# One more up-projection tile by Strassen's scheme, and coarser turns in the attention

## The chip, the cores and the metric

The kernel runs on one core of a Trainium2 chip. The metric is device time in microseconds (us), median of three runs. The core has TensorE (PE: matmuls, results in PSUM banks of 128 x 512 words), VectorE (DVE) and ScalarE (ACT, activations with a scale and a running sum), GpSimd (POOL, which here issues DMAs and does little arithmetic) and SyncE (SP, which issues the weight loads). All DMA queues share 16 DMA engines.

## What is computed

One decoder block on 512 tokens of width 1024, in float32:

```python
proj = rmsnorm(x) @ w_in
o_a = nsa_mixer(q, k_c, v_c, k_s, v_s, k_w, v_w, nsa_gate)  # 8 query heads, 2 KV groups
o_b = rwkv7_mixer(rwkv_in)
merged = sigmoid(gate_a) * (o_a @ w_proj_a) + sigmoid(gate_b) * (o_b @ w_proj_b)
x = x + merged @ w_out
u = rmsnorm(x) @ w_up                    # 1024 x 5632: value and gate, 2816 columns each
val, gate = split(causal_conv3(u))
return x + (silu(gate) * val) @ w_down
```

The attention mixer adds three branches for each query head, each with its gate: a softmax over 31 compressed blocks, one over selected tokens and one over a window; with 512 tokens the last two see every earlier token.

## The kernel before

**Numbers.** Every weight and activation is split into two parts, `hi` (rounded to TensorE's fast 32-bit type) and `lo` (the rest); a product is three matmuls: hi by hi, lo by hi, hi by lo. For each weight tile SP loads `raw` (three buffers, `wload`), ACT makes `whi`, DVE makes `wlo` (`wsplit`, two buffers each). A `raw` buffer is free, and the load of the tile three places on is issued, when `wlo` of its tile has been made. `wnext` always splits one tile ahead of the one that TensorE uses. The order of the tiles is that of the generator `weight_tiles`.

**Attention** (lines 1240 to 1411). The twelve entries of `units` are (query tile qt, KV group, branches): eight with one branch, for qt 3 and 2, and four with both, for qt 1 and 0. `scores(u)` makes the scores of four heads in groups of one PSUM bank (tag `a`, two buffers): TensorE writes `ps_a`, DVE adds the bias table and takes the maximum (line 1314, output `P`, `nm`), ACT takes the exponential. The generator yields after each group; before the yield it issues DVE's pending scalings of the unit before (`pend`, one piece per group: rows of `P` times `sm`, line 135) and `filler(n)` matmuls of the two dense projections (`obT`, weights `w_proj_b`), which keep TensorE busy. `turns(u)` transposes the finished `P` in sets of four 128 x 128 blocks (line 1349) into one of three banks and copies each set out (`PTs`), three by ACT to one by DVE. The main loop alternates: one set of transposes of unit j, one group of scores of unit j + 2. Then `values` multiplies by V. `compressed(qt)` is the compressed branch's softmax: eight small matmuls (`KC`), ten steps of DVE on `sC` and an exponential; `compressed_t` transposes it. The order of TensorE's and GpSimd's instructions is that of the code here; DVE's and ACT's is chosen when the program is built.

**Merge** (after line 1415). For m in 0 to 7, TensorE multiplies `oaT` by one 128-column tile of `w_proj_a` (12 matmuls); then comes `w_out`.

**MLP** (from line 1515). 22 tiles f of 128 value and 128 gate columns. A dense tile is 2 x 24 matmuls of 128 x 512. For f in `SF` (4 to 15) `up_strassen` uses seven products of half size in place of eight, 7 x 12 matmuls of 128 x 256 (line 1613). It needs two kinds of sums. Sums of weight blocks are formed beforehand in memory, `usum`, by `sums_in_memory` on GpSimd's queue during the attention: 16 copies (line 243) and 16 accumulating DMAs (line 246), each over the `SF` columns of 128 rows. Sums of token blocks, `up_tokens` (tiles `Hw`, split into `R1M` and `R3Q`), are made by DVE and ACT while the dense tiles f = 0 to 3 run, two steps per tile. The first products of a Strassen tile need, in this order, the blocks H00 and H01 of the plain activations, then M2, R1 and R3 of the sums.

The functions that the change touches:

Of the kernel before, what the change touches and what calls it, by code (L numbers as in the profile page):

```python
# [22 lines left out]
KT = D // 128  # L23
DH = 64
H = 8
# [10 lines left out]
NGA = 1  # L36
NGB = 7
DECAY = math.exp(-0.5)
SF = range(4, 16)

O_Q, O_KC, O_VC, O_KS, O_VS, O_KW, O_VW, O_GATE, O_RWKV, O_GA, O_GB = (
    0, 512, 640, 768, 896, 1024, 1152, 1280, 1304, 3096, 4120)
# [42 lines left out]
def hybrid_block(ctx: ExitStack, tc: tile.TileContext, A: dict, out: bass.AP):  # L85
# [164 lines left out]
    def weight_tiles():  # L250
# [48 lines left out]
        for f in list(SF) + [None]:  # L299
# [8 lines left out]
                stream.append(up_block(p, 1, 1))  # L308
            if f is not None:
                stream += [up_sum(f, TS1), up_sum(f, TS3)]  # L310
        for i in range(0, len(stream) - 2, 2):
            yield stream[i:i + 2], KT, 128, v
        yield cols(A["w_up"][0], DFF + 128 * (SF[-1] + 1))
        yield stream[-2:], KT, 128, v
# [978 lines left out]
    def scores(u, n):  # L1293
        qt, g, bs = u
        qs = slice(128 * qt, 128 * qt + 128)
        N = 128 * (qt + 1)
        B = len(bs)
        P = Pb[units.index(u) % 4][:, 0:4 * B * N].rearrange("p (b r n) -> p b r n", b=B, n=N)
        nm = at.tile([128, 8], F32, name="nm", tag="nm", bufs=2)
        sm = at.tile([128, 8], F32, name="sm", tag="sm", bufs=2)  # L1300
        per = 512 // (B * N)
        todo, pend[:] = list(pend), []
        ng = 4 // per
        for r0 in range(0, 4, per):
            sp = pa()[:, 0:per * B * N].rearrange("p (r b n) -> p r b n", r=per, b=B)
            for r in range(r0, r0 + per):
                h = 4 * g + r
                for i, K in enumerate((KH, KL)):
                    mm(sp[:, r - r0], qst[:, h, qs], K[:, bs[0]:bs[0] + B, g, 0:N], i == 0, i == 1)
            for r in range(r0, r0 + per):  # L1310
                h = 4 * g + r
                for b in range(B):
                    i = 4 * b + r
                    v.tensor_tensor_reduce(out=P[:, b, r], in0=sp[:, r - r0, b], in1=BT[:, h, 384 - 128 * qt:512],  # L1314
                                           scale=-1.0, scalar=-NEG, op0=ALU.add, op1=ALU.min, accum_out=nm[:, i:i + 1])
                    act(P[:, b, r], P[:, b, r], AF.Exp, scale=-1.0, bias=nm[:, i:i + 1], accum_out=sm[:, i:i + 1])
            ig = r0 // per
            for f in todo[len(todo) * ig // ng:len(todo) * (ig + 1) // ng]:
                f()
            filler(n * (r0 + per) // 4 - n * r0 // 4)  # L1320
            yield
        v.reciprocal(sm[:, 0:4 * B], sm[:, 0:4 * B])
        for x, b in enumerate(bs):
            tt(sm[:, 4 * x:4 * x + 4], sm[:, 4 * x:4 * x + 4], gts[:, qt, 12 * g + 1 + b:12 * g + 12:3], ALU.mult)
        def row(b, r):
            i = 4 * b + r
            if r == 3:
                act(P[:, b, r], P[:, b, r], AF.Copy, scale=sm[:, i:i + 1])
            else:
                ts(P[:, b, r], P[:, b, r], sm[:, i:i + 1], None)  # L1330

        def branch(b):
            tt(P[:, b], P[:, b], sm[:, 4 * b:4 * b + 4, None].to_broadcast([128, 4, N]), ALU.mult)

        if B > 1:
            pend.append(lambda: branch(1))
        pend.extend(lambda r=r: row(0, r) for r in range(4))
        Ps[u] = P
# [50 lines left out]
    with tc.manual_schedule(engines=KTS):  # L1389
        run(scores(units[0], 12))  # L1390
        compressed(3)
        run(scores(units[1], 16))
        for i in range(0, len(units), 2):
            if i in (4, 8, 10):
                compressed_t(units[i][0])
            for j in (i, i + 1):
                a, b = turns(units[j]), scores(units[j + 2], nfill[j]) if j + 2 < len(units) else dense_only(nfill[j])
                alive = [a, b]
                while alive:
                    for x in list(alive):  # L1400
                        if next(x, alive) is alive:
                            alive.remove(x)
                    if j == 1 and len(PTk[units[1]]) == 2:
                        compressed_t(3)
            for j in (i, i + 1):
                values(units[j])
            for j in (i, i + 1):
                output(units[j])
            if i in (0, 4, 6):
                compressed({0: 2, 4: 1, 6: 0}[i])  # L1410
        filler(100)
    dbg("oaT", oaT.bitcast(F32))

# [185 lines left out]

    wpart = []  # L1600

    def up_weight():
        if not wpart:
            hi, lo = wnext(KT, 128)
            wpart.extend((hi[:, 4 * i:4 * i + 4], lo[:, 4 * i:4 * i + 4]) for i in range(2))
        return wpart.pop(0)

    def up_product(bank_, x, first=False):

        hi, lo = up_weight()  # L1610
        for k in range(8):
            for y in x[:2 - k // 4]:
                te.matmul(bank_, lhsT=(hi, lo)[k // 4][:, k % 4], rhs=y[:, k % 4], start=first and k == 0 and y is x[0],  # L1613
# [15 lines left out]
    def up_strassen():  # L1629
# [4 lines left out]
        for f in list(SF) + [None]:  # L1634
            if f is not None:
                B1 = mmb()[:, b0]
                up_product(B1, H[0][0], True)
                u = [us[:, 3 * (f % 2) + k] for k in range(3)]
                Cg, Cv = craw[f % 2], craw[2 + f % 2]
                act(u[0], B1)  # L1640
# [29 lines left out]
    for f in range(NF):  # L1670
# [15 lines left out]
        if f // 2 < PD:  # L1686
            cv = conv(dense_fm(hh, hl) if f else lead[1], f, 2 + f % 2)
            gate_value(f, cg, cv)
            for _ in range(2):
                next(side, None)  # L1690
            continue
        act(cg, cg, AF.Silu)
# [232 lines left out]
```

## Time and profile before

| what | us |
|---|---|
| median of three runs | 803.11 (802.75 to 803.26) |
| the profiled execution | 802.89 |
| its span, first to last instruction | 801.1 |
| outside the span | 1.8 |
| TensorE busy | 790.1 |
| VectorE busy | 642.1 |
| ScalarE busy | 482.8 |
| TensorE's granted clock | 1.00 throughout (2.4 GHz) |

Times in rows are microseconds from the span's start. Matmuls overlap: the length of one reaches into the next, so what an instruction costs is read from the distance of two starts. The same holds for DVE and ACT, whose lengths contain some 0.08 us of overlap. The attention runs from about 296 to 390 us, the merge to 412, the MLP from 459.

### The profile page before, as it was taken

The page shows a single profiled execution, that of the slowest core. Times are in us where ns is not written, and L with a number is a line of the kernel's source. Part 1 is how long each engine was busy: PE and PEld are TensorE (multiplying, and loading weights), DVE is VectorE, ACT ScalarE, POOL GpSimd, SP SyncE. Part 2 cuts the span into 40 slices and gives each one's busy share as a digit, 9 for nine tenths or more (in the row PEclk, how much of TensorE's full clock was granted, in tenths as well). Part 3 has the DMA queues.
Part 4 walks back from the last instruction along what each step waited for, and adds up shares of the span by engine and source line. Part 5 has one row for each costly group of instructions (what it writes and reads, how often), then busy time and mean ns, then how long its engine had stood idle before and what let it go on. Part 6 is the DMA issues. An engine that isn't in the chain of part 4 may idle for free.

```text
span 801.1 us, 14229 instructions
## 1 busy us (share of the span) xinstructions
PE 790.1 (99%) x5439; PEld 668.5 (83%) x5439; DVE 642.1 (80%) x1179; ACT 482.8 (60%) x929; POOL 92.8 (12%) x125
## 2 busy tenths in 40 slices
PE   7999999999999999999999999999999999999998
PEld 6788888887777887877788888999999888888886
DVE  4688899974565679888585489688898999989997
ACT  6777765454455678787344366677777754553452
POOL 5300021142000052221000000000000000002101
PEclk9999999999999999999999999999999999999999
DMA  7432323337362389999957134566666422584654
GB/s 221 125 90 68 99 74 105 86 101 210 80 132 54 79 227 271 261 261 269 196 183 243 50 133 118 154 185 182 173 184 182 128 79 80 181 309 167 234 179 153
DMA packets 138185, 126.27 MB, mean 158 GB/s; under 512 B 5806, under 2 KB 116069, under 8 KB 137989
## 3 DMA queue, kind: packets, MB, share of 16 engines
q1 hardware_dynamic: 123744, 83.21, 36.1%
q0 software_dynamic: 13312, 39.61, 18.5%
q10 hardware_dynamic: 1060, 2.55, 1.1%
q8 instruction: 42, 0.69, 0.4%
q14 instruction: 27, 0.21, 0.1%
HBM read 119.91 MB, written 29.56 MB: 187 GB/s over the span
## 4 chain that ended last, share of the span: by engine, by line
PE 90%; DVE 4%; DMA 4%; ACT 1%; issue 0%; POOL 0%; DVEq 0%
PE ps_mm L125 60%; PE ps_mm L1613 8%; PE ps_a L125 7%; PE ps_b L125 5%; PE ps_b L1613 4%; DMA usum<-in_w_up_dram 3%; PE ps_a L1613 2%; PE ps_b L1349 1%; DVE wlo L366 1%; PE ps_mm L1349 1%; DMA kc<-in_consts_dram 1%; DVE raw L131 0%; ACT whi L128 0%; PE ps_b L404 0%; PE ps_b L663 0%
## 5 line engine op out<-in xcount | busy, mean ns | idle before, releaser
L128 ACT ACTIVATE whi<-raw 128x1024 fp32r<-128x1024 f32 (+2 forms) x148 | 147.7, 999 | 129.9 <-PE ps_mm L125 61.0
L366 DVE TENSOR_TENSOR wlo<-raw,whi 128x1024 fp32r<-128x1024 f32 (+1 forms) x133 | 152.9, 1151 | 47.0 <-ACT whi L128 27.2
L125 PE MATMUL ps_mm<-hh,whi 128*128 128x512 f32 (+1 forms) x432 | 167.7, 391 | 0.3 <-ACT whi L128 0.2
L125 PE MATMUL ps_mm<-hl,whi 128*128 128x512 f32 (+1 forms) x432 | 160.5, 383 | 0.0
L125 PE MATMUL ps_mm<-hh,wlo 128*128 128x512 f32 (+1 forms) x432 | 107.9, 382 | 0.0
L125 PEld LDWEIGHTS ps_mm<-hh,whi 128*128 128x128 f32 x432 | 81.2, 188 | 18.4 <-issue 0.8
L125 PEld LDWEIGHTS ps_mm<-hh,wlo 128*128 128x128 f32 x432 | 81.2, 188 | 16.1 <-DVE wlo L366 0.3
L125 PEld LDWEIGHTS ps_mm<-hl,whi 128*128 128x128 f32 x432 | 79.2, 188 | 15.2 <-DVE hl L140 0.3
L1754 POOL DMA_DIRECT2D cgq<-in_w_down_dram x12 | 6.4, 535 | 290.0 <-DVE cgq L131 237.0
L128 ACT ACTIVATE P<-P,nm 128x512 f32<-128x512 f32 (+3 forms) x64 | 35.4, 555 | 4.5 <-DVE nm L1314 4.1
L131 DVE TENSOR_TENSOR cgq<-cgq 128x512 f32<-128x512 f32 (+1 forms) x49 | 32.9, 672 | 1.0 <-ACT cgq L128 0.2
L1314 DVE CUSTOM_DVE_ANT_0 P<-ps_a,AB 128x512 f32<-128x512 f32 (+3 forms) x64 | 30.1, 485 | 3.0 <-PE ps_a L125 2.9
L140 DVE SCALAR_TENSOR_TENSOR cgq<-cr,cw,cgq 128x511 f32<-128x511 f32 (+1 forms) x36 | 26.9, 748 | 4.4 <-ACT cgq L128 4.0
L140 DVE SCALAR_TENSOR_TENSOR cgq<-ps_mm,cw,cgq 128x511 f32<-128x511 f32 (+1 forms) x40 | 29.6, 746 | 1.1 <-ACT cgq L128 1.0
L1613 PE MATMUL ps_mm<-hl,whi 128*128 128x256 f32 x96 | 24.1, 283 | 0.0
L1613 PE MATMUL ps_mm<-hh,whi 128*128 128x256 f32 x96 | 24.1, 283 | 0.0
L128 ACT ACTIVATE QK<-ps_mm 128x64 f32<-128x64 f32 (+5 forms) x52 | 13.4, 303 | 15.3 <-PE ps_mm L125 15.2
L125 PE MATMUL ps_mm<-whi,hh 128*128 128x280 f32 (+2 forms) x72 | 22.4, 331 | 0.0
L128 ACT ACTIVATE ring<-cgq 128x1024 fp32r<-128x1024 f32 x12 | 12.7, 1060 | 15.8 <-DVE cgq L131 15.8
L125 PE MATMUL ps_mm<-whi,hl 128*128 128x280 f32 (+2 forms) x72 | 21.9, 323 | 0.0
L128 ACT ACTIVATE cgq<-ps_mm,cw 128x512 f32<-128x512 f32 x20 | 15.4, 776 | 8.8 <-PE ps_mm L125 8.0
L125 PE MATMUL ps_mm<-obT,whi 128*128 128x512 f32 x64 | 20.2, 397 | 0.0
(539 smaller groups left out, 1933.1 us busy)
## 6 DMA issues: line engine op xcount, KB each, us to landing
raw<-in_w_in_dram SPq DMA_DIRECT2D x38, 512.0 KB, 3.9
usum<-in_w_up_dram POOLq DMA_DIRECT2D x24, 768.0 KB, 23.6
raw<-in_w_down_dram SPq DMA_DIRECT2D x25, 512.0 KB, 4.0
raw<-usum SPq DMA_DIRECT2D x48, 256.0 KB, 3.3
raw<-in_w_up_dram SPq DMA_DIRECT2D x20, 512.0 KB, 3.8
raw<-in_w_up_dram SPq DMA_DIRECT2D x36, 256.0 KB, 3.3
usum<-usum POOLq DMA_DIRECT2D x8, 768.0 KB, 23.2
cgq<-in_w_down_dram POOLq DMA_DIRECT2D x12, 512.0 KB, 4.4
```

Source lines behind the costliest of these rows:

```text
L125: te.matmul(o, lhsT=l, rhs=r, start=start, stop=stop)
L128: sc.activation(o, i, f, **kw)
L131: v.tensor_tensor(o, a, b, op=op)
L140: v.scalar_tensor_tensor(o, a, s, b, op0=op0, op1=op1)
L366: eng.tensor_tensor(lo, raw, hi.bitcast(F32), op=ALU.subtract)
L1314: v.tensor_tensor_reduce(out=P[:, b, r], in0=sp[:, r - r0, b], in1=BT[:, h, 384 - 128 * qt:512], scale=-1.0, scalar=-NEG, op0=ALU.add, op1 ...
L1349: te.transpose(pt[:, 128 * i:128 * i + 128], P[:, x, i, 128 * k:128 * k + 128], ident)
L1613: te.matmul(bank_, lhsT=(hi, lo)[k // 4][:, k % 4], rhs=y[:, k % 4], start=first and k == 0 and y is x[0], stop=k == 7, skip_group_check=n ...
L1754: nc.gpsimd.dma_start(raws[g][i], A["w_down"][0][256 * g + 128 * i:256 * g + 128 * i + 128])
```

## The change

Three things change.

1. `SF` begins at 3: thirteen tiles by Strassen's scheme. The dense tile f = 3 goes; `up_tokens` has three steps per dense tile in place of two, so that it ends a tile earlier; the DMAs of `sums_in_memory` cover 1664 columns in place of 1536. The number of weight blocks becomes odd, so the first block comes as a tile of its own, half as large (`up_weight(n)`).
2. In the attention each turn takes two sets of transposes and two groups of scores. Where a unit has only two groups (qt 0), all pending scalings of the unit before are issued after the first group.
3. `compressed(0)` is issued after the turns of unit 8 (j == 8), no longer before them.

```diff
@@ -36,7 +36,7 @@
 NGA = 1
 NGB = 7
 DECAY = math.exp(-0.5)
-SF = range(4, 16)
+SF = range(3, 16)
 
 O_Q, O_KC, O_VC, O_KS, O_VS, O_KW, O_VW, O_GATE, O_RWKV, O_GA, O_GB = (
     0, 512, 640, 768, 896, 1024, 1152, 1280, 1304, 3096, 4120)
@@ -308,7 +308,8 @@
                 stream.append(up_block(p, 1, 1))
             if f is not None:
                 stream += [up_sum(f, TS1), up_sum(f, TS3)]
-        for i in range(0, len(stream) - 2, 2):
+        yield stream[:1], 4, 128, v
+        for i in range(1, len(stream) - 2, 2):
             yield stream[i:i + 2], KT, 128, v
         yield cols(A["w_up"][0], DFF + 128 * (SF[-1] + 1))
         yield stream[-2:], KT, 128, v
@@ -1315,7 +1316,7 @@
                                            scale=-1.0, scalar=-NEG, op0=ALU.add, op1=ALU.min, accum_out=nm[:, i:i + 1])
                     act(P[:, b, r], P[:, b, r], AF.Exp, scale=-1.0, bias=nm[:, i:i + 1], accum_out=sm[:, i:i + 1])
             ig = r0 // per
-            for f in todo[len(todo) * ig // ng:len(todo) * (ig + 1) // ng]:
+            for f in todo[len(todo) * ig // ng:len(todo) * (ig + 1) // ng] if ng > 2 else todo[5 * ig:5 * (ig + 1)]:
                 f()
             filler(n * (r0 + per) // 4 - n * r0 // 4)
             yield
@@ -1398,16 +1399,18 @@
                 alive = [a, b]
                 while alive:
                     for x in list(alive):
-                        if next(x, alive) is alive:
+                        if any(next(x, alive) is alive for _ in range(2)):
                             alive.remove(x)
                     if j == 1 and len(PTk[units[1]]) == 2:
                         compressed_t(3)
+                if j == 8:
+                    compressed(0)
             for j in (i, i + 1):
                 values(units[j])
             for j in (i, i + 1):
                 output(units[j])
-            if i in (0, 4, 6):
-                compressed({0: 2, 4: 1, 6: 0}[i])
+            if i in (0, 4):
+                compressed({0: 2, 4: 1}[i])
         filler(100)
     dbg("oaT", oaT.bitcast(F32))
 
@@ -1599,15 +1602,15 @@
 
     wpart = []
 
-    def up_weight():
+    def up_weight(n=2):
         if not wpart:
-            hi, lo = wnext(KT, 128)
-            wpart.extend((hi[:, 4 * i:4 * i + 4], lo[:, 4 * i:4 * i + 4]) for i in range(2))
+            hi, lo = wnext(4 * n, 128)
+            wpart.extend((hi[:, 4 * i:4 * i + 4], lo[:, 4 * i:4 * i + 4]) for i in range(n))
         return wpart.pop(0)
 
-    def up_product(bank_, x, first=False):
-
-        hi, lo = up_weight()
+    def up_product(bank_, x, first=False, n=2):
+
+        hi, lo = up_weight(n)
         for k in range(8):
             for y in x[:2 - k // 4]:
                 te.matmul(bank_, lhsT=(hi, lo)[k // 4][:, k % 4], rhs=y[:, k % 4], start=first and k == 0 and y is x[0],
@@ -1634,7 +1637,7 @@
         for f in list(SF) + [None]:
             if f is not None:
                 B1 = mmb()[:, b0]
-                up_product(B1, H[0][0], True)
+                up_product(B1, H[0][0], True, 1 if f == SF[0] else 2)
                 u = [us[:, 3 * (f % 2) + k] for k in range(3)]
                 Cg, Cv = craw[f % 2], craw[2 + f % 2]
                 act(u[0], B1)
@@ -1686,7 +1689,7 @@
         if f // 2 < PD:
             cv = conv(dense_fm(hh, hl) if f else lead[1], f, 2 + f % 2)
             gate_value(f, cg, cv)
-            for _ in range(2):
+            for _ in range(3 if f < SF[0] else 2):
                 next(side, None)
             continue
         act(cg, cg, AF.Silu)
```


TensorE before, where unit 8 (tile `P_3385`) is transposed and unit 10 is scored (`KH`, `KL`); `KC` is `compressed(0)`, `sC` a transposed compressed softmax, `obT` the filler:

```order
L125 MATMUL ps_a<-KC,qst 128x64 x8
L1290 MATMUL ps_a<-kc,sC_3375 128x128 x2
L1349 MATMUL ps_b<-kc,P_3385 128x128 x4
L125 MATMUL ps_a<-KH,qst 128x256
L125 MATMUL ps_a<-KL,qst 128x256
L125 MATMUL ps_a<-KH,qst 128x256
L125 MATMUL ps_a<-KL,qst 128x256
L125 MATMUL ps_mm<-obT,wlo 128x512 x3
L125 MATMUL ps_mm<-obT,whi 128x512 x2
L1349 MATMUL ps_mm<-kc,P_3385 128x128 x4
L125 MATMUL ps_a<-KH,qst 128x256
```

And with the change, from the filler behind the first of the two groups of scores to the first two sets of unit 9 (`P_3386`):

```order
L125 MATMUL ps_mm<-obT,wlo 128x512 x3
L125 MATMUL ps_mm<-obT,whi 128x512 x2
L125 MATMUL ps_a<-KH,qst 128x256
L125 MATMUL ps_a<-KL,qst 128x256
L125 MATMUL ps_a<-KH,qst 128x256
L125 MATMUL ps_a<-KL,qst 128x256
L125 MATMUL ps_mm<-obT,whi 128x512 x6
L1350 MATMUL ps_b<-kc,P_3385 128x128 x8
L125 MATMUL ps_a<-KC,qst 128x64 x8
L1350 MATMUL ps_mm<-kc,P_3386 128x128 x4
L1350 MATMUL ps_b<-kc,P_3386 128x128 x4
```

The eight `KC` matmuls have moved from ahead of unit 8's transposes to behind them, and unit 9's first two sets stand together.

VectorE before, while the token sums are made (`R1M`, `R3Q`: lo parts of the sums; `wlo`: splits of weights; `cgq`: convolution and gate):

```order
L131 TENSOR_TENSOR R1M_5123<-Hw,R1M_5123 128x1024
L131 TENSOR_TENSOR a2a_pairs<-cgq,a2a_pairs 128x256
L366 TENSOR_TENSOR wlo<-raw,whi 128x1024
L140 SCALAR_TENSOR_TENSOR cgq<-ps_mm,cw,cgq 128x511
L366 TENSOR_TENSOR wlo<-raw,whi 128x1024
L140 SCALAR_TENSOR_TENSOR cgq<-ps_mm,cw,cgq 128x510
L131 TENSOR_TENSOR R1M_5123<-Hw,R1M_5123 128x1024
L131 TENSOR_TENSOR R3Q<-Hw,R3Q 128x1024
L140 SCALAR_TENSOR_TENSOR cgq<-ps_mm,cw,cgq 128x511
L366 TENSOR_TENSOR wlo<-raw,whi 128x1024
L140 SCALAR_TENSOR_TENSOR cgq<-ps_mm,cw,cgq 128x510
```

And with the change, up to the split of the second Strassen weight tile, the last row (128x1024; the 128x512 split is the first, half-size one):

```order
L140 SCALAR_TENSOR_TENSOR cgq<-ps_mm,cw,cgq 128x510
L131 TENSOR_TENSOR R1M_5123<-Hw,R1M_5123 128x1024
L131 TENSOR_TENSOR cgq<-cgq 128x512
L131 TENSOR_TENSOR R3Q<-Hw,R3Q 128x1024
L131 TENSOR_TENSOR a2a_pairs<-cgq,a2a_pairs 128x256
L367 TENSOR_TENSOR wlo<-raw,whi 128x1024
L140 SCALAR_TENSOR_TENSOR cgq<-ps_mm,cw,cgq 128x511
L367 TENSOR_TENSOR wlo<-raw,whi 128x512
L140 SCALAR_TENSOR_TENSOR cgq<-ps_mm,cw,cgq 128x510
L131 TENSOR_TENSOR R3Q<-Hw,R3Q 128x1024
L140 SCALAR_TENSOR_TENSOR cgq<-ps_mm,cw,cgq 128x511
L367 TENSOR_TENSOR wlo<-raw,whi 128x1024
```

Ahead of these twelve rows, with the change, stand from the step `a<-cgq` on: an `Hw` step, a convolution step of 511 or 510 columns, an `Hw` step, a convolution step, a `wlo` split of 1024, a convolution step, an `R1M` step. The splits of weights now stand behind sums that before came between later tiles. On TensorE, the eight hi products with the first half-size weight tile stand ahead of the eight `wlo` products of the last dense tile.

GpSimd's DMA issues before (a copy, then sums; the order of copies and sums is the same throughout):

```order
L243 DMA usum<-in_w_up_dram 128x1536
L246 DMA usum<-usum 384x512
L243 DMA usum<-in_w_up_dram 128x1536
L246 DMA usum<-in_w_up_dram 128x3x512
L243 DMA usum<-in_w_up_dram 128x1536
```

And with the change:

```order
L243 DMA usum<-in_w_up_dram 128x1664
L246 DMA usum<-usum 416x512
L243 DMA usum<-in_w_up_dram 128x1664
L246 DMA usum<-in_w_up_dram 128x4x416
L243 DMA usum<-in_w_up_dram 128x1664
```

A source row that was three pieces of 512 words is four of 416; a sum from `usum` has 416 pieces in place of 384.

## Rows read from the trace of the kernel before

**Rows 1.** The page, part 1: busy us, share of the span, instructions, by engine.

```profile
PE 790.1 (99%) x5439; PEld 668.5 (83%) x5439; DVE 642.1 (80%) x1179; ACT 482.8 (60%) x929; POOL 92.8 (12%) x125
```

**Rows 2.** The chain of waits: start, length, work, instructions, in the MLP's first half.

```profile
520.21 2.88 PE ps_mm L1613 x24
...
628.64 77.76 PE ps_mm L125 x342
```

**Rows 3.** Timeline of TensorE in the first transpose turns: start, length, instruction.

```profile
308.40 0.60 PE L1349 MATMUL ps_b<-kc,P 128*128 128x128 f32 x4
308.75 0.49 PE L125 MATMUL ps_a<-KH,qst 128*128 128x512 f32 x1
309.08 0.40 PE L125 MATMUL ps_a<-KL,qst 128*128 128x512 f32 x1
```

**Rows 4.** Timeline of TensorE where the ninth unit's transposes run.

```profile
364.55 0.60 PE L1349 MATMUL ps_b<-kc,P 128*128 128x128 f32 x4
365.19 0.39 PE L125 MATMUL ps_a<-KH,qst 128*128 128x256 f32 x1
...
369.21 1.03 PE L1349 MATMUL ps_b<-kc,P 128*128 128x128 f32 x8
370.08 0.27 PE L1349 MATMUL ps_mm<-kc,P 128*128 128x128 f32 x1
371.47 0.70 PE L1349 MATMUL ps_mm<-kc,P 128*128 128x128 f32 x3 [1.12 <-DVE P L135]
```

**Rows 5.** Timeline of VectorE ahead of that wait's end.

```profile
365.07 0.42 DVE L131 TENSOR_TENSOR sC<-ps_a,BC 128x256 f32<-128x256 f32 x1
...
370.73 0.43 DVE L131 TENSOR_TENSOR sC<-sC,mx 128x256 f32<-128x256 f32 x1
371.06 0.61 DVE L135 TENSOR_SCALAR P<-P,sm 128x256 f32<-128x256 f32 x2
```

**Rows 6.** DMA issues of `raw` at 369.5, 392.2, 401.4: count, size, us to landing.

```profile
raw<-in_w_proj_a_dram SPq DMA_DIRECT2D x1, 256.0 KB, 11.9
...
raw<-in_w_proj_a_dram SPq DMA_DIRECT2D x1, 256.0 KB, 6.0
...
raw<-in_w_proj_a_dram SPq DMA_DIRECT2D x1, 256.0 KB, 2.6
```

**Rows 7.** Timeline of GpSimd's DMA issues: the first copies and the last sum.

```profile
286.28 2.11 POOL L243 DMA_DIRECT2D usum<-in_w_up_dram  x4
...
389.14 0.95 POOL L246 DMA_DIRECT2D usum<-usum  x1 [9.33 <-DMA usum<-usum]
```

**Rows 8.** DMA issues from 389 to 398 us: the last sum.

```profile
usum<-usum POOLq DMA_DIRECT2D x1, 768.0 KB, 8.4
```

**Rows 9.** Timelines of VectorE, ScalarE and TensorE at the fifth `w_proj_a` tile.

```profile
391.43 0.68 DVE L366 TENSOR_TENSOR wlo<-raw,whi 128x512 fp32r<-128x512 f32 x1
...
398.26 0.63 ACT L128 ACTIVATE whi<-raw 128x512 fp32r<-128x512 f32 x1 [1.98 <-DMA raw<-in_w_proj_a_dram]
...
401.22 1.07 PE L125 MATMUL ps_mm<-oaT,whi 128*128 128x512 f32 x4
```

**Rows 10.** Timeline of VectorE while the MLP's token sums are made.

```profile
480.36 0.42 DVE L131 TENSOR_TENSOR a<-cgq,a 128x256 fp32r<-128x256 f32 x1
...
485.27 0.74 DVE L140 SCALAR_TENSOR_TENSOR cgq<-ps_mm,cw,cgq 128x510 f32<-128x510 f32 x1
485.93 1.22 DVE L140 SCALAR_TENSOR_TENSOR Hw<-Hw 128x1024 f32<-128x1024 f32 x1
487.06 0.69 DVE L131 TENSOR_TENSOR cgq<-cgq 128x512 f32<-128x512 f32 x1
...
488.80 0.42 DVE L131 TENSOR_TENSOR a2a_pairs<-cgq,a2a_pairs 128x256 fp32r<-128x256 f32 x1
```

**Rows 11.** Timeline of TensorE in the last projection of the third MLP tile.

```profile
491.52 1.98 PE L125 MATMUL ps_mm<-hh,wlo 128*128 128x512 f32 x8
493.34 0.39 PE L125 MATMUL ps_mm<-hh,whi 128*128 128x512 f32 x1
```

## The prediction

> **What bounds the kernel now.** I read the page's shares first: TensorE is busy for 790.1 of the span's 801.1 us [rows 1], at full clock throughout. A gain can therefore come from fewer or cheaper TensorE instructions, or from the 11 us in which it waits; a loss from any new wait. Next the chain of waits, for what a TensorE instruction costs in the MLP: a Strassen product piece is 2.88 us for 24 matmuls, 0.12 each, and dense matmuls take 77.76 us for 342, 0.2274 each [rows 2]. Then TensorE's timeline in the attention, for the places where the next start comes later than the work explains [rows 3, 4], VectorE's timeline ahead of the one large wait [rows 5], and last the DMA issues and the other engines where the change puts more work: merge [rows 6 to 9] and the start of the Strassen tiles [rows 10, 11].
>
> **One Strassen tile more.** A dense tile is 48 matmuls: 48 x 0.2274 = 10.91 us. By Strassen's scheme it is 84 of half width: 84 x 0.12 = 10.08. The gain on TensorE is 0.83 us, no more. The tile also takes more VectorE and ScalarE work, which in the later tiles lies beside TensorE's 10 us per tile; I cost it at nothing there. At its start it is not hidden, which comes next.
>
> **The start of the Strassen tiles.** With three steps per dense tile the order puts more VectorE work ahead of the split of the second Strassen weight tile, the one with H01 and M2. Before, the step `a<-cgq` ends at about 480.36 + 0.35 = 480.71 [rows 10]. From there to the end of that split the changed order has nineteen instructions: nine of 1024 columns (1.13 from start to next start, 485.93 to 487.06), seven convolution steps (0.66, 485.27 to 485.93), one multiplication (0.69 - 0.08 of overlap = 0.61), one `a2a` step (0.34), and the half-size split of 512 (0.60, from 0.68 in [rows 9]). That is 10.17 + 4.62 + 0.61 + 0.34 + 0.60 = 16.34, so the split ends at 497.05 if VectorE never waits. TensorE: the last dense projection's eight `wlo` matmuls begin at 491.52 and end at 493.34 [rows 11]. The new order puts eight half-width products of H00 ahead of them (0.96), so they end at 494.30; the rest of H00 (four, 0.48) ends at 494.78 and the eight hi products of H01 (0.96) at 495.74. Then TensorE needs the split: a stall of 1.3 us. Queued behind it are the products of M2 and all that follows. It stays if VectorE is busy throughout, and shrinks to 0 if ScalarE and VectorE come out 1.3 us better than these steps. I take 1.3, bounds 0 and 1.5. The MLP's net is then -0.83 + 1.3 = +0.5, between -0.8 and +0.7.
>
> **The attention's grouping.** What does alternating cost TensorE? A set of four transposes followed by scores takes 0.35 to the next start, the first KH after it 0.33 where a matmul of that width in a row takes 0.23, so a switch pair costs 0.35 + 0.33 - 0.23 = 0.45 [rows 3]. Eight transposes in a row take 0.87, or 0.435 per set [rows 4]. Joining two sets saves 0.02 us, perhaps a dozen times: 0.2 at most, and I take 0. Against it, a bank of scores is wanted back sooner; the groups of two come with the same filler behind each, so I take 0 with an upper bound of 0.4, the wait of 0.29 below being the nearest row.
>
> **The later compressed softmax.** At unit 9 TensorE does one transpose at 370.08, due to be followed at 370.19, and the next begins at 371.47: 1.28 us lost, to VectorE's scaling of `P` [rows 4]. VectorE did the ten steps on `sC` between 365.07 and 371.06 [rows 5], 2.6 us of it (about seven of 0.33 and three small ones). Without them ahead, the rows of `P` that were scaled by 371.67 are ready by about 369.1, and since the scalings now come after the first group rather than spread over two, sooner still; they are due at 370. Just before, a set of transposes begun at 364.55 is followed by scores only at 365.19, 0.64 later where 0.35 would do [rows 3, 4]: 0.29, which I put down to the banks that `KC` and `sC` hold. Both waits go: -1.5, bounds -1.1 (the second stays, some of the first returns) and -1.9. The eight `KC` matmuls are only moved, and the step issues no DMA, so no queue is moved past. What is late next: the ten steps now fall beside unit 10's rows and ahead of `compressed_t(0)`. The rows of unit 10 have a turn of filler and two sets of unit 9's transposes more before they are due; I cost that at 0, and at 1.3, the wait removed, if the cover is not there.
>
> **The sums in memory.** Each copy and sum is 1664 columns in place of 1536. They run from 286.28 to the landing of the last sum, 389.14 + 8.4 = 397.5 [rows 7, 8]: 111.2 us, and each waits for an earlier one. If their time goes with bytes (13/12), the end moves by 9.3 us to 406.8. If it goes with pieces, the 24 copies and sums from `usum` grow by 13/12 and the 8 sums from `w_up` by 4/3: mean 1.146, +16.2, end 413.7. The Trainium skill's page "DMA: Bandwidth & Descriptors", section "Anatomy of one DMA — SWDGE (gpsimd) path", puts a DMA at 2.0 us and bytes over 436 GB/s, so it would have the cost go by bytes; the rows of before do not decide between the two.
>
> This matters to the merge, since a `raw` load under the sums is slow: 256 KB took 11.9 us at 369.49, 6.0 at 392.18 with one sum left, and 2.6 at 401.4 with none [rows 6]. The fifth `w_proj_a` tile is the tight one. Its load was issued at 392.18, behind `wlo` of the tile three ahead (391.43 + 0.68); it landed for `whi` at 398.26, which took 0.63, so done at 398.89, and TensorE wanted it at 401.22 [rows 9]. Slack 2.3, so a latency of 6.0 + 2.3 = 8.3 is free. With the attention 1.5 us earlier that load is issued at about 390.7, and needed 1.5 earlier too, so the 8.3 stays. But the sums then stand where they stood earlier before: by bytes at 390.7 - 9.3 = 381.4, by pieces at 374.5. Between 11.9 at 369.49 and 6.0 at 392.18 a straight line gives 8.8 and 10.6. The stall is 0.5 or 2.3; I take 1.2, a little nearer to bytes, with bounds 0 and 3.6 (11.9 - 8.3). The tiles behind it are issued later, when less of the sums is left, and are pushed back by the same stall, so I take nothing more, and up to 1 for the first tiles of `w_out`. By the skill's formula alone (same section) a 256 KB load would take 2.6 us and there would be no stall; the 2.6 agrees with the row without sums and not with the two under them.
>
> **Sum.** Attention -1.5, merge +1.2, MLP +0.5: +0.2 on the profiled execution's own 802.89 (span 801.1 and 1.8 around it). That execution lies 0.2 below the median of 803.11. On the median's scale: 803.3.
>
> **The rivals.** (a) The loads do not become late: the sums slow each other rather than the loads. For it: 2.6 us is all a load needs alone, and SP's queue is not GpSimd's. Against it: 11.9 under the sums. Then -1.5 + 0.5 = -1.0, 802.1; with the MLP's stall gone as well 803.1 - 1.5 - 0.8 = 800.8. The skill's formula above is on this side. (b) The sums cost by pieces or worse and the loads take the full 11.9 through the merge: 3.6 at the fifth tile in place of 1.2, or +2.4, and `w_out` late by up to 1: 803.3 + 2.4 to 3.4, about 806. It decides from a latency of 8.3 us on; against it is that 6.0 was seen as soon as one sum was left. (c) The attention's wait moves and does not go: the coarser turn or the ten steps make unit 10 wait instead. Then the 1.5 is not gained: 804.8. Against it is that unit 10's rows are due a whole turn later. (d) The change in the attention does nothing because the switches cost nothing; as far as the grouping alone goes that is my forecast, but the moved step stands in DVE's way at one known place, so this is (c) again.
>
> **How the numbers follow.** My forecast's case (attention's gain mostly given back in merge and MLP, 801.7 to 804.6) has 0.50; (a) 0.22, of which half with the MLP's stall gone; (b) 0.14; (c) 0.14. What a measurement of this kernel can tell from no change is about 0.2%, 1.6 us: 801.5 to 804.7. (a) at 800.8 and a small part of my own case give faster, 0.17; half of (c), all of (b) and a tenth of my own case give slower, 0.25; the rest is the same, 0.58. The range leaves out the ends of (a) and (b): 800.9 to 806.0.
>
> **What would show it.** Right: no wait over 0.3 us on TensorE between unit 8 and unit 10; the last sum landing after 405 us; a TensorE wait of 0.5 to 2.3 us for `whi` at the fifth `w_proj_a` tile, released by the DMA; a wait of about 1.3 for `wlo` among H01's products; 84 half-width matmuls more and 48 dense ones fewer. Wrong: no wait in the merge, with `raw` landing in under 8 us (then it is faster), new waits on scores' banks or on `P` in the attention, or waits at more than one tile of the merge (then it is slower).

## The result and the profile after

The changed kernel takes **809.70 us** (median of 6 runs, 807.44 to 810.68), against 802.95 for the one before in the same runs: a ratio of 1.0081, 95% interval 1.0067 to 1.0095. By the medians it is 6.75 us slower. The prediction was 803.3, range 800.9 to 806.0. The profiled execution took 808.92, span 807.1.

The page of the changed kernel says that TensorE is busy for as long as before [rows 1], in a span that is 6 us longer:

```profile
PE 789.7 (98%) x5475; PEld 669.0 (83%) x5475; DVE 643.4 (80%) x1184; ACT 484.7 (60%) x935; POOL 93.4 (12%) x125
```

So waits were added. To place them, both profiled executions are cut at TensorE's first matmul on `oaT`, its first and last on `mTh`, and the last Strassen product. Lengths in us, from the starts in the traces:

| stretch | before | after | difference | forecast |
|---|---|---|---|---|
| start to merge | 390.29 | 388.37 | -1.92 | -1.5 |
| merge | 21.81 | 26.64 | +4.83 | +1.2 |
| `w_out` | 45.10 | 45.99 | +0.89 | 0 |
| end of `w_out` to last Strassen product | 171.15 | 172.58 | +1.43 | +0.5 |
| rest | 172.72 | 173.55 | +0.83 | 0 |

The last row lies between 172.8 and 173.4 in the profiles of the other kernels with thirteen tiles, so none of its +0.83 is shown to belong to the change. The merge, too, varies from execution to execution: in e4 below, whose code is the changed kernel's up to there, it took 29.54. With the long sums it is longer than before in every profile (25.11 in e2, 26.30 in e6), but one execution gives its size only to some 3 us.

The merge first. The waits of TensorE from 385 to 418 us, by what was waited for; the kernel before has no row in this view:

```profile
PE ps_mm L125 <- ACT whi L128: 2.9, 2, 2.5
PE ps_mm L125 <- DVE wlo L367: 0.7, 2, 0.3
PE ps_mm L125 <- DVE ta L140: 0.6, 1, 0.6
```

TensorE's timeline there. The fifth tile, which began at 401.22 in [rows 9], would follow the row at 398.39 by 0.9 us; it comes 2.6 us late, the seventh waits too, and each time the lo matmuls wait once more for their split:

```profile
398.39 1.07 PE L125 MATMUL ps_mm<-oaT,wlo 128*128 128x512 f32 x4
401.94 2.12 PE L125 MATMUL ps_mm<-oaT,whi 128*128 128x512 f32 x8 [2.48 <-ACT whi L128]
404.40 1.20 PE L125 MATMUL ps_mm<-oaT,wlo 128*128 128x512 f32 x4 [0.33 <-DVE wlo L367]
...
408.75 2.14 PE L125 MATMUL ps_mm<-oaT,whi 128*128 128x512 f32 x8 [0.39 <-ACT whi L128]
411.20 1.21 PE L125 MATMUL ps_mm<-oaT,wlo 128*128 128x512 f32 x4 [0.32 <-DVE wlo L367]
...
417.14 0.50 PE L125 MATMUL ps_mm<-whi,mTh 128*128 128x512 f32 x1 [0.62 <-DVE ta L140]
```

ScalarE, which makes `whi`, was itself waiting for the load:

```profile
401.26 0.63 ACT L128 ACTIVATE whi<-raw 128x512 fp32r<-128x512 f32 x1 [6.27 <-DMA raw<-in_w_proj_a_dram]
```

The DMA issues of these loads, at 390.25, 396.98 and 404.41 us, and the last sum, at 397.68 (count, size, us to landing):

```profile
raw<-in_w_proj_a_dram SPq DMA_DIRECT2D x1, 256.0 KB, 10.9
...
raw<-in_w_proj_a_dram SPq DMA_DIRECT2D x1, 256.0 KB, 11.0
...
raw<-in_w_proj_a_dram SPq DMA_DIRECT2D x1, 256.0 KB, 4.3
...
usum<-usum POOLq DMA_DIRECT2D x1, 832.0 KB, 10.0
```

The last sum lands at 397.68 + 10.0 = 407.7; before it was 397.5 [rows 7, 8]. Three loads of the merge take 11 us (the third was issued at 392.89), one of them issued 0.7 us ahead of the last sum, and the load at 404.41 lands 1.1 us after that sum. In the kernel before, the load of 6.0 us [rows 6] landed at 398.2, 0.6 us after the last sum: it was short because the sums ended, as a table further down bears out.

The second place is the first Strassen tile. TensorE's timeline:

```profile
501.05 0.74 PE L1616 MATMUL ps_a<-hh,wlo 128*128 128x256 f32 x4 [1.35 <-DVE wlo L367]
...
505.03 1.21 PE L1616 MATMUL ps_mm<-R3Q,whi 128*128 128x256 f32 x8 [0.36 <-ACT us L128]
```

The first is the wait that was forecast, for the split of the second weight tile. The second was not: TensorE waits for ScalarE's `us`. ScalarE's timeline shows why that is late: it stands behind a `whi` that waits for its load.

```profile
503.03 1.06 ACT L128 ACTIVATE whi<-raw 128x1024 fp32r<-128x1024 f32 x1 [1.84 <-DMA raw<-in_w_up_dram]
...
504.61 0.36 ACT L128 ACTIVATE us<-ps_mm 128x256 f32<-128x256 f32 x1
```

The loads of that tile went out from 497.41 on, just behind the late half-size split, which VectorE did from 496.66 to 497.34 and which frees their buffer.

### The profile page after: what moved, and what is told of

It reads as the page before. It is cut to its first block, busy times and chain, and to the rows that moved or that the text cites. A ratio compares the mean times of both kernels' runs of the same rounds, so it can differ in the third digit from the quotient of the medians.

```text
span 807.1 us, 14324 instructions
## 1 busy us (share of the span) xinstructions
PE 789.7 (98%) x5475; PEld 669.0 (83%) x5475; DVE 643.4 (80%) x1184; ACT 484.7 (60%) x935; POOL 93.4 (12%) x125
## 4 chain that ended last, share of the span: by engine, by line
PE 87%; DMA 5%; DVE 5%; ACT 2%; issue 1%; DVEq 0%; SPq 0%; ACTq 0%
PE ps_mm L125 55%; PE ps_mm L1616 8%; PE ps_a L125 7%; PE ps_b L125 5%; PE ps_b L1616 4%; DMA raw<-in_w_proj_a_dram 3%; PE ps_a L1616 2%; DMA raw<-in_w_down_dram 2%; DVE wlo L367 1%; PE ps_b L1350 1%; ACT whi L128 1%; DMA raw<-in_w_up_dram 1%; PE ps_mm L1350 1%; DVE cgq L140 1%; DMA kc<-in_consts_dram 1%
## 5 line engine op out<-in xcount | busy, mean ns | idle before, releaser
L367 DVE TENSOR_TENSOR wlo<-raw,whi 128x1024 fp32r<-128x1024 f32 (+1 forms) x135 | 154.8, 1148 | 46.4 <-ACT whi L128 28.5
L125 PE MATMUL ps_mm<-hh,whi 128*128 128x512 f32 (+1 forms) x416 | 161.5, 391 | 0.3 <-ACT whi L128 0.2
L125 PE MATMUL ps_mm<-hl,whi 128*128 128x512 f32 (+1 forms) x416 | 154.2, 382 | 0.0
L125 PE MATMUL ps_mm<-hh,wlo 128*128 128x512 f32 (+1 forms) x416 | 104.0, 382 | 0.0
L125 PEld LDWEIGHTS ps_mm<-hh,whi 128*128 128x128 f32 x416 | 78.2, 188 | 17.7 <-issue 0.8
L125 PEld LDWEIGHTS ps_mm<-hh,wlo 128*128 128x128 f32 x416 | 78.1, 188 | 15.5 <-DVE wlo L367 0.3
L125 PEld LDWEIGHTS ps_mm<-hl,whi 128*128 128x128 f32 x416 | 76.2, 188 | 14.5 <-DVE hl L140 0.3
L140 DVE SCALAR_TENSOR_TENSOR cgq<-ps_mm,cw,cgq 128x511 f32<-128x511 f32 (+1 forms) x36 | 26.6, 746 | 0.8 <-ACT cgq L128 0.7
L1616 PE MATMUL ps_mm<-hl,whi 128*128 128x256 f32 x104 | 26.1, 283 | 0.0
L1616 PE MATMUL ps_mm<-hh,whi 128*128 128x256 f32 x104 | 26.1, 283 | 0.0
L1616 PEld LDWEIGHTS ps_mm<-hl,whi 128*128 128x128 f32 x104 | 20.0, 192 | 0.1
```

The source lines that it names most:

```text
L125: te.matmul(o, lhsT=l, rhs=r, start=start, stop=stop)
L140: v.scalar_tensor_tensor(o, a, s, b, op0=op0, op1=op1)
L367: eng.tensor_tensor(lo, raw, hi.bitcast(F32), op=ALU.subtract)
```

## The experiments

Each kernel was timed against the one before (medians 802.7 to 802.8 in these runs); ratios are to it, with 95% intervals. Theory A: the longer sums make the merge wait, and the attention's part is a gain of its own. Theory B: the merge's tiles come when the DMAs allow, and what the attention gains is waited for there.

**e1: the attention's part alone.** Twelve tiles, with the edits of the attention from the change.

> The attention's part of the change alone (coarser turns, the later compressed softmax, the pending scalings); twelve Strassen tiles and the sums as before. Theory A (the merge waits because the sums in memory last 10 us longer; the attention's part by itself is a gain of 1.9 us, seen as the start of the last values 374.8 against 376.7): about 801.1, no wait over 0.3 us in the merge, since the sums land at 397.5 as before. Theory B (the loads of the merge are bound by the DMAs, so whatever the attention gains is waited for in the merge): a wait of about 1.9 us at the fifth tile of the merge, and 803.0.

Measured 801.24 (800.93 to 802.46), ratio 0.9979 (0.9970 to 0.9988). A holds here: the gain is kept when the sums end as before. The profiled execution (802.30) has a single wait of 0.3 us up to the merge's end, and a merge of 22.71, 0.9 more than before, so little slack is left.

**e2: the Strassen part alone.**

```diff
-                        if any(next(x, alive) is alive for _ in range(2)):
+                        if next(x, alive) is alive:
...
-                if j == 8:
-                    compressed(0)
...
-SF = range(4, 16)
+SF = range(3, 16)
```

(The first lines against the changed kernel, the last two against the one before; the pending scalings are undone too, and `compressed(0)` stands where it stood.)

> The thirteenth Strassen tile alone, with its longer sums and three token steps per dense tile; the attention as before. Theory A (a load under the sums takes some 11 us wherever it stands, so the merge's waits do not depend on when the attention ends): the merge loses 5 to 6 us again, and the time is the changed kernel's plus the attention's 1.9: about 811.5. Theory B (the end of the sums sets when the merge's tiles arrive, and the attention's gain is lost in waiting for them): the merge loses 1.9 less, about 3.8, and the time is that of the changed kernel, 809.7.

Measured 808.08 (807.00 to 808.50), ratio 1.0060 (1.0047 to 1.0072). That is 1.6 below theory B's number and 3.4 below A's. TensorE's waits from 385 to 418 us in this kernel:

```profile
PE ps_mm L125 <- ACT whi L128: 1.4, 1, 1.4
PE ps_mm L125 <- DVE wlo L367: 0.7, 2, 0.3
PE ps_mm L125 <- DVE ta L140: 0.3, 1, 0.3
```

The merge begins 1.8 us later than in the changed kernel (390.17) and `w_out` 0.3 us later (415.28 against 415.01). The 0.3 by itself would be thin: the last sum lands at 406.0 here and at 407.7 in the changed kernel's profile, and in e4, with the same code up to there, at 409.8. The medians carry the reading: without the attention's gain of 1.6 us (e1) this kernel takes no longer than the changed one. Where the sums are long, that gain is waited for. So neither theory holds alone: the sums are the cause, and they also take the attention's gain. A second thing is seen here, in the loads issued at 392.06 and 394.69 us:

```profile
raw<-in_w_proj_a_dram SPq DMA_DIRECT2D x1, 256.0 KB, 8.4
...
raw<-in_w_proj_a_dram SPq DMA_DIRECT2D x1, 256.0 KB, 10.8
```

The later one, nearer to the end of the sums, took longer.

**e3: the sums as short as before.** The changed kernel with the copies and sums cut to 1536 columns; the thirteenth tile's own sums are left out, and it reads those of the twelfth. (The accumulating DMAs and the reading are cut in the same way, not shown.)

```diff
+    NS = 128 * (len(SF) - 1)
...
-                nc.gpsimd.dma_start(usum[t][128 * k:128 * k + 128], up_rows(*ij, k))
+                nc.gpsimd.dma_start(usum[t][128 * k:128 * k + 128, 0:NS], up_rows(*ij, k))
```

> The changed kernel, but the DMAs of the sums in memory cover 1536 columns as before; the sums of the thirteenth tile are left out, and it reads those of the twelfth. Theory A (the longer sums alone make the merge wait): the sums land at about 397.5, the merge's waits of 5.7 us go, and the time is about 804.0, of which 1.2 is the start of the Strassen tiles. A rival (the merge waits because TensorE and the loads of the raw tiles meet otherwise after the coarser turns): the waits stay, about 809.

Measured 802.84 (802.41 to 804.06), ratio 1.0000 (0.9992 to 1.0009). The merge takes 21.81 again, without a wait. The load issued at 390.3 us, where the changed kernel's took 10.9:

```profile
raw<-in_w_proj_a_dram SPq DMA_DIRECT2D x1, 256.0 KB, 7.1
```

That is the strongest single result: 128 columns of sums, one in thirteen, carry the whole loss of 0.8%. What is left of the change cancels: -1.86 up to the merge and +1.76 from `w_out` to the last Strassen product. The pieces of a sum from `w_up` are 512 words again here, so that bytes and pieces go back together; e6 changes the pieces alone.

**e4: Q's token step later.** Two steps per dense tile again, the last behind the first R3 product.

```diff
-            for _ in range(3 if f < SF[0] else 2):
+            for _ in range(2):
...
+                if f == SF[0]:
+                    assert next(side, 0) == 0
                 act(u[2], B1, AF.Copy, scale=-1.0)
```

> The changed kernel with two token steps per dense tile as before; the last step, that of Q, comes only after the first R3 product. The splits of the first Strassen weight tiles then stand further ahead on VectorE. Theory A (VectorE's token steps ahead of the splits, and the late loads behind these splits, cost 2 us at the start of the Strassen tiles): the waits of 1.5 and 0.5 us there go, 807.7. A rival (the raw tiles arrive too late there in any case, because their buffers come free late): the wait for the third weight tile stays or grows, 809 or more.

Measured 807.55 (806.11 to 809.16), ratio 1.0055 (1.0043 to 1.0068). The median agrees with theory A's 807.7, but the runs spread by 3 us (in the profiled one, 809.16, the clock fell in the merge; see the last section). The stretch up to the last Strassen product tells more: 171.54 against 172.58. The waits are more than halved, not gone, so theory A holds in part:

```profile
PE ps_a L1616 <- DVE wlo L367: 0.5, 1, 0.5
PE ps_mm L1616 <- ACT us L128: 0.2, 1, 0.2
```

**e5: the sums earlier.** The first four copies behind the second exchange of keys.

```diff
             nc.gpsimd.dma_start(KL[o, b, g], KL[i, b, g])
+            if b == 0 and g == 0:
+                sums_in_memory(True)
```

> The changed kernel with the first four copies of the sums issued behind the first two exchanges of keys on GpSimd's queue in place of behind the eighth, so about 279.6 in place of 286.3. Theory A (the merge waits for as long as the sums still run): the last sum lands about 5 us earlier, at some 402 to 403, the merge's waits shrink by half or more, 805 to 806.5. A rival (the sums are bound by their own chain of waits, and the keys and the w_proj_b tiles come late behind the copies): the sums end as before, or TensorE waits at the start of the attention, 809 or more.

Measured 805.65 (804.96 to 807.02), ratio 1.0034 (1.0021 to 1.0047). Only the place of four DMAs on a queue was changed. The first copy goes out at 279.07, the last sum lands at 391.58 + 9.9 = 401.5, and the merge takes 23.39 in place of 26.64. Theory A's forecast came true, with the sums ending 6 us earlier and not 5.

**e6: smaller pieces.**

```diff
-                                    accum_op=ALU.add, max_dma_last_dim=2048)
+                                    accum_op=ALU.add, max_dma_last_dim=1024)
```

> The changed kernel with the accumulating DMAs cut into pieces of at most 1024 bytes in place of 2048. Theory A1 (a DMA engine alternates between the queues piece by piece, so a raw load of 512-byte rows waits for one piece of a sum per row of its own): the loads under the sums take 6.5 to 8 us in place of 10.9, the fifth tile of the merge hardly waits, and the time falls to about 804 to 806 unless the sums end over 8 us later. Theory A2 (the load's time goes with the sums' bytes in flight, whatever their pieces): 10 us and more as before, the sums end later for the smaller pieces, 810 to 814.

Measured 809.04 (808.73 to 810.04), ratio 1.0077 (1.0063 to 1.0091). DMA issues from 390 to 405 us:

```profile
raw<-in_w_proj_a_dram SPq DMA_DIRECT2D x4, 256.0 KB, 8.9
usum<-usum POOLq DMA_DIRECT2D x1, 832.0 KB, 11.8
```

The loads are shorter (8.9, where the changed kernel's four have a median of 10.9), so the size of the pieces matters, but by 2 us and not by half; and the sums end 3.7 us later (issue 399.57 + 11.8). That the two nearly cancel is read from these rows; they were not tried apart. Neither A1 nor A2 is right as stated.

**e7 and e8: the attention's part divided.** e7 has the coarser turns and the pending scalings, e8 only the moved compressed softmax; both with twelve tiles.

> Twelve Strassen tiles, the compressed softmax where it was; of the attention's part only the coarser turns and the pending scalings. By the trace of the attention's part alone, the wait in unit 1's transposes grows from 0.33 to 0.95 and the later units gain 0.5. Theory C (the gain in the attention is the moved softmax): 803.0, merge starting at about 390.2. Rival (the gain comes from the coarser turns): 801.4.

> Twelve Strassen tiles and turns of one set and one group as before; only the compressed softmax of the last query tile is issued after unit 8's turns. Theory C: the wait of 1.28 us in unit 9's transposes goes without the wait of 0.95 in unit 1, the merge starts at about 388.7, 801.2. Rival (without the scalings brought forward, unit 9's rows of P stay late): the wait stays at 0.5 to 1 us, 802.5.

Measured: e7 801.19 (800.97 to 801.95), ratio 0.9980 (0.9971 to 0.9988); e8 801.17 (800.87 to 801.73), ratio 0.9979 (0.9971 to 0.9988). Each alone brings what both bring together. Unit 9's first set in e8, and then its first two sets in e7, where [rows 4] had 1.28 us lost between 370.08 and 371.47:

```profile
369.68 0.66 PE L1349 MATMUL ps_mm<-kc,P 128*128 128x128 f32 x4
370.09 0.36 PE L125 MATMUL ps_a<-KH,qst 128*128 128x256 f32 x1
```

```profile
369.72 0.60 PE L1349 MATMUL ps_mm<-kc,P 128*128 128x128 f32 x4
370.22 0.66 PE L1349 MATMUL ps_b<-kc,P 128*128 128x128 f32 x4
```

It is one wait, and two ways of bringing the rows of `P` forward: VectorE's scaling, at 371.06 in [rows 5], begins at 367.88 in e8, and at 367.71 and 368.31 in e7, where the softmax still stands where it stood. Which of e7's two edits does it, the turns or the scalings, was not divided further.

**e9: the last sums behind the merge.** The four sums that are needed last are issued behind the merge's end. (Their collecting is not shown; the memset moves from VectorE to GpSimd.)

```diff
+    with tc.manual_schedule(engines={mybir.EngineType.Pool}):
+        nc.gpsimd.memset(xpad, 0.0)
+        for x in late_sums:
+            add_sum(x)
```

> The changed kernel, all its sums done in full, but the four sums of the kind that is needed last are issued behind the merge, beside w_out, whose tiles have rows of 2 KB. Theory A (only the sums that still run in the merge cost there): the sums ahead of the merge land by about 370, the merge takes 21.8 as before and 4.8 less than in the changed kernel; the w_out loads under the four late sums take 5 to 6 us, since a 2 KB row waits for one piece where a 512-byte row does too; w_out loses 1 at most: about 804.5. Rival (whatever stands under the sums loses the same): w_out loses what the merge gains, 808 or more.

Measured 812.71 (811.50 to 813.79), ratio 1.0123 (1.0110 to 1.0136). The merge is clear, 21.81, as A has it. `w_out` takes 55.64 in place of 45.99: the rival. Its DMA issues from 412 to 436 us:

```profile
usum<-usum POOLq DMA_DIRECT2D x4, 832.0 KB, 24.3
raw<-in_w_out_dram SPq DMA_DIRECT2D x4, 512.0 KB, 10.9
x<-in_x_dram ACTq DMA_DIRECT2D x1, 2048.0 KB, 16.4
raw<-in_w_up_dram SPq DMA_DIRECT2D x2, 512.0 KB, 13.7
```

The guess that loads with rows of 2 KB would pass in 5 to 6 us was wrong: 10.9, with four sums and `x` in flight. Part of that may be `x`: beside `x` alone, at 419.1 in the kernel before, a load of 512 KB took 9.1 us.

**e10: R3 and Q later.** e9, with one token step for the last dense tile and the two last ones among the first Strassen products.

```diff
-            for _ in range(3 if f < SF[0] else 2):
+            for _ in range(1 if f == SF[0] - 1 else 2):
...
+                if f == SF[0]:
+                    next(side)
                 up_product(B1, M2)
```

> The kernel with the four sums behind the merge, and the token steps of R3 and Q only after the first Strassen products. The theory of the token steps ahead of the splits: both waits at the start of the Strassen tiles (1.5 and 0.5 us) go, 1.4 to 2 less than the kernel with the sums moved alone: about 803, of which the thirteenth Strassen tile gains 0.8. Rival (the splits wait for the half-size tile's loads instead): less than 0.7 gained.

Measured 810.86 (808.91 to 813.08), ratio 1.0101 (1.0086 to 1.0116), 1.85 below e9, though the intervals touch. The forecast of 803 rested on e9's 804.5 and missed with it. The stretch is the better evidence: TensorE has no wait from 485 to 520 us, and the way up to the last Strassen product takes 170.34, where e9 had 172.73. That is 0.81 less than in the kernel before, which is what a thirteenth tile was worked out to save.

**e11: single turns.** e10 with turns of one set and one group.

> The kernel with the moved sums and the late R3 and Q, with turns of one set and one group as before, the compressed softmax still moved. If the coarser turns bring nothing (as the trial of each part alone showed): the same time within 0.5. If they and the softmax add up: slower by 1 or more.

Measured 809.79 (808.45 to 812.98), ratio 1.0089 (1.0074 to 1.0105). That is 1.1 below e10, outside both forecasts, but the ranges overlap widely; the merge begins at 388.38 against 388.24. So the coarser turns add nothing that shows to the moved softmax, as e7 and e8 have it.

**e12: the sums kept clear of the merge.** The changed kernel with e5's early copies, e10's late steps, and the very last sum alone behind the copy of `x1`, after `w_out`.

```diff
     with tc.manual_schedule(engines={mybir.EngineType.Pool}):
         nc.gpsimd.dma_start(x1d, x1.rearrange("p t d -> p (t d)"))
+        add_sum(TS4, 3, TS2)
```

> The changed kernel with three edits: the first four copies of the sums earlier, the very last sum alone behind the copy of x1 (after w_out, where the cores' DMAs are used least), and the steps of R3 and Q after the first Strassen products. If the merge's waits come from the sums that still run there, and the waits at the Strassen tiles from the token steps: merge 21.8, w_out 45.1, the first dense tile to the last Strassen product 0.8 less than before, 800.4, below both kernels and a little below the one with the softmax moved alone (801.17). If one sum beside the first MLP tiles costs there as four did beside w_out: 2 to 4 us more, 803 to 805.

Measured **800.72** (800.32 to 802.68), ratio 0.9975 (0.9966 to 0.9984): faster than both kernels. The late sum takes 11.4 us beside the first MLP tiles, and nothing waits for it. Its ten other runs lie within 1 us, the profiled one (802.68) above them; in that one the merge takes 22.53, `w_out` 45.39, and the way up to the last Strassen product 171.05, which is 0.1 less than before and not the 0.8 of the forecast. TensorE's waits from 385 to 520 us in it are:

```profile
PE ps_mm L1624 <- ACT us L128: 0.4, 1, 0.4
PE ps_mm L125 <- DVE wlo L371: 0.3, 1, 0.3
PE ps_mm L125 <- ACT whi L128: 0.2, 1, 0.2
```

Each taken against the kernel before in its own runs, e12 gains 1.97 us, and e7 and e8 with twelve tiles 1.65 and 1.67. The thirteenth tile is then worth 0.3 us by the medians, of the 0.83 that it saves TensorE; the intervals overlap, so that these runs do not tell the two apart. Which of its three edits clears the merge was not divided; e5 has the early copies without the other two.

## Why the prediction was wrong

**The step that failed** is the merge's: "Between 11.9 at 369.49 and 6.0 at 392.18 a straight line gives 8.8 and 10.6", with 1.2 us taken from it. Two points were joined as if a load became shorter as the sums ran out. Loads of 256 KB, by what was left of the sums when they were issued (from there to the landing of the last sum):

| kernel | load issued at | us of sums left | load took | landed after the last sum |
|---|---|---|---|---|
| before | 369.49 | 28.0 | 11.9 | |
| before | 385.21 | 12.3 | 8.3 | |
| before | 392.18 | 5.4 | 6.0 | 0.6 |
| before | 394.81 | 2.7 | 4.1 | 1.4 |
| changed | 390.25 | 17.4 | 10.9 | |
| changed | 392.89 | 14.8 | 10.9 | |
| changed | 396.98 | 10.7 | 11.0 | 0.3 |
| changed | 404.41 | 3.3 | 4.3 | 1.1 |
| e2 | 392.06 | 13.9 | 8.4 | |
| e2 | 394.69 | 11.3 | 10.8 | |
| e2 | 398.60 | 7.4 | 7.9 | 0.5 |

(The 8.3 at 385.21 is counted to the last update of the load's semaphore.) In these rows a load with more than 10 us of sums left takes 8.3 to 11.9 us, with no steady fall towards the end (e5 has one of 6.8); one with less left lands within 1.4 us of the sums' end; alone it takes 2.6. The line, at these distances from the end, gives 9.1, 8.5 and 7.4 for the changed kernel's first three loads of the merge; they took 10.9, 10.9 and 11.0. The 6.0 was the wrong point to draw through, and its "one sum left" was a misreading: the sum issued at 378.85 took 14.4 us,

```profile
usum<-usum POOLq DMA_DIRECT2D x1, 768.0 KB, 14.4
```

so that two were in flight at 392.18, and the load was short because it outlasted both. At the fifth tile the slack of 8.3 did hold: a latency of 10.9 is 2.6 over it, and the tile came 2.6 us late, where 1.2 had been taken.

**The larger part** is what stands behind it: "The tiles behind it are issued later, when less of the sums is left", so that nothing more was taken. The tiles behind waited too: the merge and `w_out` lost 4.83 + 0.89 = 5.7 us, above my bound of 3.6 + 1, and 3.1 of it lies behind the fifth tile's first wait. Rival (b), 806, had the mechanism (a latency over 8.3 that lasts through the merge) with the chance 0.14, and priced only one tile of it. The sign that I had set down for a slower kernel, waits at more than one tile of the merge, is the one that came.

**"so the 8.3 stays"** was right in arithmetic and missed its meaning. Arriving 1.5 us earlier leaves a load its slack only if the load's time is its own. Where it ends with the sums, time that TensorE gains ahead of it is waited for: with the short sums the attention's edits are worth 1.6 us (e1), with the long ones nothing (808.08 without them in e2, 809.70 with them).

**The sums' end** was right: 406.8 by bytes, 407.7 measured (406.0 in e2 and 409.8 in e4). By pieces it would have been 413.7. The Trainium skill's page "DMA: Bandwidth & Descriptors", section "Anatomy of one DMA — SWDGE (gpsimd) path", has the cost go by bytes and a fixed part, and here the trace agrees. The estimate of 2.6 us for a load of 256 KB, worked out from that fit, which the page gives for GpSimd's path and not for SP's, holds for SP's load alone and is four times too short under the sums.

**The attention** was right in size (-1.92, forecast -1.5, bound -1.9) and half right in cause. The moved softmax does remove the wait (e8); but "Joining two sets saves 0.02 us" led to a gain of 0 for the coarser turns, and with the scalings they remove the same wait (e7). I priced only what they cost TensorE and not what they move on VectorE. They also add a wait in unit 1, where I had bounded their cost by 0.4:

```profile
313.03 0.44 PE L1350 MATMUL ps_b<-kc,P 128*128 128x128 f32 x2 [0.79 <-DVE P L135]
```

TensorE does two transposes from 311.86, and the next begins at 313.03: 0.95 lost, where the kernel before lost 0.33 at this place.

**The Strassen tile** gains what was forecast (0.83; 0.81 in e10). The wait for the second split was mis-sized slightly: 1.3 forecast, 1.5 measured between starts. The step left out was what the late splits hold up in turn: buffers, so a load, so `whi`, so the `us` behind it on ScalarE, 0.5 us. That is the whole of +1.43 against +0.5 but for some 0.2 of restarts.

## What to carry to other kernels

In this case a long background transfer had no price of its own until it overlapped a place where loads have a deadline; then its end was the number to forecast, and time won ahead of that place was waited for. Compare the end with the first deadline behind it: here 10 us more of a transfer that nobody waits for cost 5.7 us, and moving its start by 7 us and one piece to a later place brought them back (e12). Of two samples of a latency, ask what ended each before a line is drawn through them.

## What was not expected of the hardware

TensorE's clock can fall after waits of this size, from 1.00 (2.4 GHz) to 0.50 (1.2 GHz). In e9 the windows of six microseconds from 434 on, and a shorter one inside them (busy us of PE, PEld, DVE, ACT and POOL, granted clock, DMA share, GB/s):

```profile
434.00:440.00 6.00, 2.71 (x8) 1.91 (x9) 3.36 (x4) 2.72 (x6) 0.00 (x0) 0.77 1.12 227
440.00:446.00 6.00, 6.00 (x20) 4.77 (x19) 0.29 (x1) 0.00 (x0) 0.00 (x0) 0.67 1.11 230
446.00:452.00 6.00, 6.00 (x28) 4.98 (x27) 3.00 (x4) 2.65 (x4) 0.00 (x0) 1.00 0.67 194
...
438.00:443.00 5.00, 4.52 (x11) 3.59 (x12) 1.82 (x2) 1.05 (x3) 0.00 (x0) 0.50 1.13 213
```

After TensorE had waited in more than half of the first window, the second, in which it was busy throughout, was granted 0.67 of full speed on the average: 20 matmuls in place of the 28 of the third. So part of e9's loss in `w_out` is the clock's and not the loads'.

The merge's waits can do the same. In the changed kernel's profiled execution the clock stayed at 1.00 there. In e4's, where the code up to there is the same, TensorE waited for a fifth time, the clock fell, and eight matmuls took 3.41 us to the next start, in place of the 1.82 of eight at 0.2274:

```profile
410.77 3.57 PE L125 MATMUL ps_mm<-oaT,whi 128*128 128x512 f32 x8 [1.68 <-ACT whi L128]
414.18 1.09 PE L125 MATMUL ps_mm<-oaT,wlo 128*128 128x512 f32 x4
...
412.00:418.00 6.00, 6.00 (x23) 4.81 (x23) 6.00 (x10) 3.02 (x4) 0.00 (x0) 0.84 0.45 140
```

The other five runs of the changed kernel, of which there is no trace, have a mean granted clock of 0.997 to 0.999 over the whole span, the profiled one 1.000 and e4's 0.997. So some of the 809.70 may be the clock's as well; how much is not shown.
